# Merged rows to channels: transfers ahead of weight loads, turning ahead of splits, and one step a piece later

## The chip, the cores and the metric

The kernel runs on one core of one Trainium2 chip. The metric is the time of one execution on the device in microseconds (us). Three executions of the kernel before took 885.33, 885.78 and 892.01 us; their median is 885.78 us. A separate execution was profiled, and all rows and durations below come from that one.

## The reference: what is computed

Two layers, each with two halves, on 256 tokens of 1024 channels in float32. The first half mixes tokens:

```python
def _token_mixer(xn, ...):
    u, q, k, v, g_pool, g_attn = jnp.split(xn @ w_in, SPLITS, axis=-1)
    pool_out = ...        # centred means of u in 4 windows, minus u, times w_pool, times pool_scale
    attn_out = ...        # 12 heads in 3 dilated groups, merged by their softmax denominators
    merged = jax.nn.sigmoid(g_pool) * (pool_out @ w_a) + jax.nn.sigmoid(g_attn) * (attn_out @ w_b)
    return merged @ w_o

h = h + _token_mixer(_rmsnorm(h, norm1[layer]), ...)
h = h + _conv_ffn(_rmsnorm(h, norm2[layer]), w_up, conv_w, conv_b, w_down)
```

The second half is a gated MLP of width 2816 with a convolution over three tokens. At the end stands one more RMSNorm. The change lies between `merged` and `merged @ w_o`, with one small edit a little before it.

## The kernel before

**Three products for one.** Every float32 operand of a matmul is split into a high part, which ScalarE (ACT) makes by a cast, and a low part, which VectorE (DVE) makes by subtracting the high part from the operand. The product is then high by high, high by low and low by high, all on TensorE (PE). So each weight that arrives from memory has to pass ACT (line L194, tiles `wh`) and DVE (line L195, tiles `wl`) before PE can use it.

**The stream of weights.** The class `Weights` holds two lists that are laid out ahead of time: *loads*, each a transfer of 1 MB that SyncE (SP) issues (L131, tiles `raw`), and *pieces*, each half a load, in the order in which PE uses them. The raw tiles have three buffers, so a load has to wait until DVE has split both pieces of the load three places earlier. The split tiles have five buffers, so a split has to wait until PE is done with the piece five places earlier. Some pieces go to tiles that lie idle then (`slots`), such as the first three pieces of `w_up` (tiles `v1`, `ybig` and `at2`). `get` hands out the next piece and splits ahead by three.

In layer 0 the pieces around the change are: 62 to 65 (the first half of the attention gate's weights), 66 and 67 (`w_b`, first half), 68 to 71 (second half of the gate's), 72 and 73 (`w_b`, second half), 74 to 81 (`w_o`, eight chunks of 128 rows), and from 82 on `w_up`. Loads 37 to 40 are those of `w_o`, load 41 is the first of `w_up`. Layer 1 has the same order.

**What orders the work.** The order of instructions on each engine is settled when the program is built, by a scheduler that follows the order of the code and its own estimates; an engine then runs its list in order, and an instruction that waits holds up all that stand behind it on that engine. `issue_after(x)` makes what is traced in its block stand behind `x` in the list of the engine of `x`, and does nothing on other engines. `queue_behind(insts, n, first)` does that for the splits of `n` pieces from `first` on. SP's list holds all transfers, loads and others.

**From merged rows to channels.** `merged` comes out with tokens on the partitions, and `w_o` needs channels on the partitions. The second loop over `HALVES` does this for 512 channels at a time (n = 0 and n = 1). PE computes the gate (`gate`, L640, four pieces) and `attn_out @ w_b` (L640, two pieces held, first the rows t = 0, then t = 1). For each t DVE multiplies by the gate (L1129), adds the pool branch (L1132) and turns blocks of 32 by 32 (L661). `to_chunks` then stores the turned rows to memory (one transfer, L668, 512 KB, tile `turned`) and fetches them back in four transfers of 128 KB with channels on partitions (L671, tile `merged`). The first of the four waits for the store to land. ACT and DVE split the result into `m` (L677 and L678, two instructions each).

In n = 1 DVE's three steps stand behind the last L678 of n = 0 (`issue_after(last[1].ins)`).

**The product with `w_o`.** `residual_mm` (L558, L559, L560) takes chunks 0 to 3, which come from n = 0, for all four output tiles. Chunks 4 to 7, which come from n = 1, are held and worked off tile by tile: rows t = 0 with columns 0 to 511, t = 0 with the rest, then t = 1. After each tile DVE adds it to `h` (L418), and ACT takes the sum of squares (L420). When t = 0 is complete, POOL finishes the norm, DVE scales (L445), and PE turns the normed rows (L454, tile `xt_ps`); this stands in PE's list after the third tile and the first 256 columns of the fourth. Then comes the first product with `w_up`, which uses pieces 82 to 85 (`begin_mlp`).

**The steps between pieces.** The attention of the last two heads is cut into six steps: scores, turn, scores, weigh, turn, weigh. They are put between the eight pieces of `pool_out @ w_a` (L1100, by `places`), one after each piece but the two named there.

Of the kernel before, what the change touches and what calls it, by code (L numbers as in the profile page):

```python
# [94 lines left out]
class Weights:  # L95
# [8 lines left out]
    def __init__(self, tc, pool, idle):  # L104
        self.tc, self.nc, self.pool, self.idle = tc, tc.nc, pool, idle
        self.loads, self.pieces = [], []
        self.n_loaded, self.n_split, self.n_got = 0, 0, 0
        self.raw, self.split = {}, {}
        self.live = set()
        self.behind, self.later = (), []  # L110
        self.n_scaled, self.gains = 0, None

    def add(self, src, shape, cuts, tag=None):
# [9 lines left out]
    def load(self, upto):  # L123
        while self.n_loaded < min(upto, len(self.loads)):
            src, shape, tag = self.loads[self.n_loaded]
            name = f"raw{self.n_loaded}"
            if tag is None:
                t = self.pool.tile([P, *shape], F32, tag="raw", bufs=self.RAW, name=name)
            else:
                t = self.idle.tile([P, *shape], F32, tag=tag, name=name)  # L130
            self.last = self.nc.sync.dma_start(out=t, in_=src)  # L131
            self.raw[self.n_loaded] = t
            self.n_loaded += 1

# [89 lines left out]
def encoder(ctx, tc, x, w_in, w_pool, pool_scale, w_a, w_b, w_o, norm1, norm2, w_up, conv_w,  # L224
            conv_b, w_down, rel_bias, norm_f, onehot, edges, out):
    nc = tc.nc
# [9 lines left out]
    W = Weights(tc, wpool, big)  # L236
# [8 lines left out]
    def rows(w, r0, n=2, c0=0, width=1024, tag=None, pieces=2):  # L245

        src = w[r0 : r0 + n * P, c0 : c0 + width].rearrange("(k p) c -> p k c", p=P)
        h = n // pieces
        return W.add(
            src, (n, width), [((lambda t, j=j: t[:, j * h : (j + 1) * h, :]), (h, width)) for j in range(pieces)],  # L250
            tag,
        )

    first_up = []
    for l in range(DEPTH):
        for g in range(NG):
            c0 = C_V + g * 512
            slots = (("m2", 0, 2), ("m2", 1, 2), ("ybig",), ("at2",)) if g == 0 else ()
            for j in range(2):
                tag = "k1" if l == 0 and g == 1 and j == 0 else None  # L260
                W.use(rows(w_in[l], j * 512, 4, c0, 512, tag), slots[2 * j : 2 * j + 2])
        if l == 0:
            W.n_scaled = len(W.pieces)
        for c in range(3, -1, -1):
            W.use(cols(w_in[l], c * 256))
        for n, c in enumerate(PAIRS):
            pool = ([], [])
            if n == 1:
                pool = W.add(
                    w_pool[l].rearrange("g (k p) c -> p (g k) c", p=P), (8, 256),  # L270
                    [((lambda t, j=j: t[:, 4 * j : 4 * j + 4, :]), (4, 256)) for j in range(2)],
                )
                pool = (pool[:1], pool[1:])
            W.use(pool[0] + cols(w_in[l], C_Q + c * 256))
            W.use(pool[1] + cols(w_in[l], C_K + c * 256))
        for w, c0 in ((w_a[l], 0), (w_in[l], C_GP)):
            for c in (c0, c0 + 512):
                W.use(rows(w, 0, 4, c, 512) + rows(w, 512, 4, c, 512))
        for c in (0, 512):
            W.use(rows(w_in[l], 0, 4, C_GA + c, 512) + rows(w_in[l], 512, 4, C_GA + c, 512))  # L280
            W.use(rows(w_b[l], 0, 4, c, 512))
        for c in range(4):
            W.use(rows(w_o[l], c * 256))
        first_up.append(len(W.pieces))
        slots = (("v1",), ("ybig",), ("at2",))
        for j in range(2):
            W.use(rows(w_up[l], j * 512, 4, 0, 512), slots[2 * j : 2 * j + 2])
        for f in range(0, NF, 2):
            a = cols(w_up[l], f * P) if f >= ENTRY else []
            g = cols(w_up[l], DFF + f * P)  # L290
            W.use([a[0], g[0], a[1], g[1]] if a else g)
            if f >= LAG:
# [338 lines left out]
    def v_tile():  # L631
        return acc.tile([P, 512], F32, tag="acc", name="v_ps")
# [12 lines left out]
    def by_tokens(x2, n, at_once=1, then=None):  # L645

        ps = [mmp.tile([P, 512], F32, tag="mm", name="t_ps") for _ in range(2)]
        for i0 in range(0, n, at_once):
            held = [W.get() for _ in range(at_once)]
            for t in range(2):  # L650
                for i, piece in enumerate(held, i0):
                    v_sum(ps[t], x2, t, i, piece, n - 1)
            for i, _ in held:
                W.free(i)
            if then:
                then()
        return ps
# [5 lines left out]
    def to_chunks(y, z, x2):  # L663

        d = dram.tile([P, 4, 256], F32, tag="turned", bufs=2, name="turned")
        nc.sync.dma_start(out=d, in_=y.rearrange("p q c t j -> p q (c t j)"))  # L668
        for q in range(4):
            src = d[:, q].rearrange("(a i) x -> i a x", a=4)  # L670
            nc.sync.dma_start(out=z[32 * q : 32 * q + 32].rearrange("p a c t j -> p a (c t j)"), in_=src)  # L671
        for c in range(0, 4, 2):
            cs = slice(c, c + 2)
            src = z[:, :, cs].rearrange("p a c t j -> p a (c t) j")
            hi, lo = (p[:, cs].rearrange("p c t (a j) -> p a (c t) j", a=4) for p in x2)
            last = (
                nc.scalar.copy(out=hi, in_=src),  # L677
                nc.vector.tensor_sub(out=lo, in0=src, in1=hi.bitcast(F32)),  # L678
            )
        return last  # L680

    def two_parts(tag, name):

# [176 lines left out]
    for l in range(DEPTH):  # L860
# [25 lines left out]
        else:  # L886
            for g in range(NG):
                held = begun[0] if g == 0 else [W.get() for _ in range(4)]
                for t in range(2):
                    if g + t == 0:  # L890
                        ps = begun[1]
                    else:
                        ps = v_tile()
# [18 lines left out]
        for gi in range(3, -1, -1):  # L912
# [10 lines left out]
            cur, n = u, S + 2 * PAD  # L923
            sh = 1
            while sh < w:
# [3 lines left out]
                    out=nxt[:, :, 0:n], in0=cur[:, :, 0:n], in1=cur[:, :, sh : sh + n]  # L929
# [7 lines left out]
            if hw > 1:  # L937
# [5 lines left out]
                out=pd, in0=cur[:, :, o : o + S], scalar=1.0 / w, in1=u[:, :, PAD : PAD + S],  # L943
# [35 lines left out]
        q = big.tile([P, NH - HPG, 2, P], F32, tag="q1", name="q")  # L979
# [72 lines left out]
        for pair in ((0, 1), (2, 3)):  # L1052
            a, b = pair
            steps += [(scores, a), (turn, a), (scores, b), (weigh, a), (turn, b), (weigh, b)]

        def step():
            if steps:
                f, hh = steps.pop(0)
                f(hh)


        for m, c in enumerate(PAIRS):
            if m == 1:
                po2 = two_parts("m2", "po2")
# [5 lines left out]
            for n in range(4):  # L1070
                if m == 1:
                    next(pool_parts)
                src, rest = (halves(a) for a in proj(x2, 1 + (m != 1)))
                hd = 2 * c + n % 2
                scale = HD**-0.5 if n < 2 else 1.0
                if hd < HPG:
# [3 lines left out]
                        out=lo[:, hd], in0=src, scalar=scale, in1=hi[:, hd].bitcast(F32),  # L1080
# [3 lines left out]
                        out=lo[:, hd], in0=rest, scalar=scale, in1=lo[:, hd].bitcast(F32),  # L1084
                        op0=ALU.mult, op1=ALU.add,
                    )
                else:
# [3 lines left out]
                        out=o, in0=src, scalar=scale, in1=o, op0=ALU.mult, op1=ALU.add  # L1091
# [5 lines left out]
        pa = big.tile([P, 2, D], F32, tag="ybig", name="pa")  # L1097
        places = iter(range(KD))
        for cc in HALVES:
            ps = by_tokens(po2, 4, then=lambda: step() if next(places) not in (1, 6) else None)  # L1100
            for t in range(2):
                nc.scalar.copy(out=pa[:, t, cc], in_=ps[t])
        assert not steps
# [9 lines left out]
        for cc in HALVES:  # L1113
            th = gate()
            for t in range(2):
                nc.vector.scalar_tensor_tensor(
                    out=pa[:, t, cc], in0=th[:, t], scalar=1.0, in1=pa[:, t, cc],
# [3 lines left out]
        mh, ml = m2[:, 0], m2[:, 1]  # L1121
        z = big.tile([P, 2, 4, 4, 2, 32], F32, tag="q1", name="merged")
        for n, cc in enumerate(HALVES):
            th = gate()
            ps = by_tokens(at2, 2, 2)
            y = big.tile([P, 4, 4, 2, 32], F32, tag=("q0", "k0")[n], name="turned")
            for t in range(2):
                with tc.issue_after(last[1].ins) if n else ExitStack():
                    nc.vector.scalar_tensor_tensor(  # L1129
                        out=th[:, t], in0=th[:, t], scalar=1.0, in1=ps[t], op0=ALU.add, op1=ALU.mult  # L1130
                    )
                    nc.vector.tensor_add(out=th[:, t], in0=th[:, t], in1=pa[:, t, cc])  # L1132
                    turned = turn_blocks(y, t, th[:, t])
                last = (None, turned)
            ks = slice(4 * n, 4 * n + 4)
            last = to_chunks(y, z[:, n], (mh[:, ks], ml[:, ks]))
            if n == 0:

                W.queue_behind(last, 5, first_up[l] - 5)
        W.queue_behind((turned,), 4, first_up[l] - 4)  # L1140
        W.queue_behind(last, 4, first_up[l])

        x2 = two_parts("x", "x2")
        norm = Norm(to_channels(x2, acc, g2))
# [40 lines left out]
        held, ps = entry  # L1185
        first = keep_entry(ps)
        ps = v_tile()
# [6 lines left out]
        last = keep_entry(ps)  # L1194
# [99 lines left out]
```

## Time and profile before

| | us |
|---|---|
| median of three executions (lowest, highest) | 885.78 (885.33, 892.01) |
| the profiled execution | 887.53 |
| its span, first to last instruction | 885.7 |
| PE busy in the span | 868.5 |
| DVE busy | 661.9 |
| ACT busy | 509.3 |
| mean granted TensorE clock | 0.992 |

The profiled execution lasted 1.83 us longer than its span; that part lies outside of the first and last instruction. Times in the rows are counted from the start of the span. Rows of the timeline have the start, the duration, the engine, the line, the operation and the tiles written and read; in brackets stands the idle time before it and what ended that. Rows of the chain of work that ended last have the start, the share of that step in the chain, and what it is. A row of the waits names who waited, for whom, the total, how often, and the longest. Matmuls overlap: one of 512 columns is shown with 0.39 us, but the next starts 0.23 us later.

### The profile page before, as it was taken

The page shows a single profiled execution, that of the slowest core. Times are in us where ns is not written, and L with a number is a line of the kernel's source. Part 1 is how long each engine was busy: PE and PEld are TensorE (multiplying, and loading weights), DVE is VectorE, ACT ScalarE, POOL GpSimd, SP SyncE. Part 2 cuts the span into 40 slices and gives each one's busy share as a digit, 9 for nine tenths or more (in the row PEclk, how much of TensorE's full clock was granted, in tenths as well). Part 3 has the DMA queues.
Part 4 walks back from the last instruction along what each step waited for, and adds up shares of the span by engine and source line. Part 5 has one row for each costly group of instructions (what it writes and reads, how often), then busy time and mean ns, then how long its engine had stood idle before and what let it go on. Part 6 is the DMA issues. An engine that isn't in the chain of part 4 may idle for free.

```text
span 885.7 us, 12137 instructions
## 1 busy us (share of the span) xinstructions
PE 868.5 (98%) x4583; PEld 748.1 (84%) x4583; DVE 661.9 (75%) x1070; ACT 509.3 (57%) x847; POOL 31.0 (3%) x98
## 2 busy tenths in 40 slices
PE   9999999999899999999999999999997999999997
PEld 7888888888688888888888888988885888888886
DVE  7998786656669978878756988764556698887884
ACT  7657554544447766666545575454444477666663
POOL 1800000000010000000000000000000100000000
PEclk9999999999989999999999999999998999999999
DMA  9676544456745475465636474544576356646531
GB/s 332 236 236 219 179 156 161 142 178 207 257 142 191 143 229 198 145 235 192 236 120 233 148 237 145 172 160 143 190 235 194 127 181 219 209 145 234 192 142 48
DMA packets 116547, 165.86 MB, mean 187 GB/s; under 512 B 3640, under 2 KB 84224, under 8 KB 116488
## 3 DMA queue, kind: packets, MB, share of 16 engines
q1 hardware_dynamic: 116328, 164.81, 55.6%
q8 instruction: 36, 0.59, 0.3%
q10 hardware_dynamic: 160, 0.27, 0.1%
q14 instruction: 23, 0.19, 0.1%
HBM read 161.90 MB, written 3.17 MB: 186 GB/s over the span
## 4 chain that ended last, share of the span: by engine, by line
PE 92%; DMA 4%; DVE 2%; SPq 1%; ACT 1%; issue 0%; POOLq 0%; POOL 0%; ACTq 0%
PE proj_ps L516 45%; PE t_ps L640 14%; PE v_ps L640 6%; PE res_ps L558 6%; PE res_ps L559 6%; PE res_ps L560 6%; DMA merged<-turned 2%; PE v_ps L852 2%; PE pool_ps L516 1%; PE v_ps L759 1%; DMA turned<-turned 1%; PE pt_ps L1022 1%; PE o_ps L1043 1%; PE s_ps L993 1%; PE s_ps L988 1%; PE o_ps L1039 1%
## 5 line engine op out<-in xcount | busy, mean ns | idle before, releaser
L195 DVE TENSOR_TENSOR wl<-raw,wh 128x1024 fp32r<-128x1024 f32 x274 | 333.5, 1221 | 138.8 <-ACT wh L194 93.7
L194 ACT CAST wh<-raw 128x1024 fp32r<-128x1024 f32 x274 | 286.2, 1050 | 133.5 <-PE t_ps L640 60.2
L516 PE MATMUL proj_ps<-x,wh 128*128 128x512 f32 x1152 | 274.5, 390 | 0.0
L516 PEld LDWEIGHTS proj_ps<-x,wh 128*128 128x128 f32 x1152 | 213.1, 188 | 42.2
L516 PEld LDWEIGHTS proj_ps<-x,wl 128*128 128x128 f32 x1152 | 144.9, 191 | 3.6
L516 PE MATMUL proj_ps<-x,wl 128*128 128x256 f32 x1152 | 147.9, 283 | 0.0
L640 PE MATMUL t_ps<-wh,x 128*128 128x512 f32 x256 | 79.6, 390 | 0.0
L558 PE MATMUL res_ps<-wh,actq 128*128 128x512 f32 (+1 forms) x184 | 70.0, 380 | 0.0
L559 PE MATMUL res_ps<-wl,actq 128*128 128x512 f32 (+1 forms) x184 | 69.9, 380 | 0.0
L560 PE MATMUL res_ps<-wh,actk 128*128 128x512 f32 (+1 forms) x184 | 69.9, 380 | 0.0
L640 PEld LDWEIGHTS t_ps<-wh,x 128*128 128x128 f32 x256 | 48.1, 188 | 10.0
L640 PE MATMUL t_ps<-wl,x 128*128 128x512 f32 x128 | 49.8, 389 | 0.0
L640 PE MATMUL t_ps<-wh,po 128*128 128x512 f32 x128 | 42.7, 399 | 0.0
L558 PEld LDWEIGHTS res_ps<-wh,actq 128*128 128x128 f32 x184 | 34.6, 188 | 6.6
L559 PEld LDWEIGHTS res_ps<-wl,actq 128*128 128x128 f32 x184 | 34.6, 188 | 6.6
L560 PEld LDWEIGHTS res_ps<-wh,actk 128*128 128x128 f32 x184 | 34.6, 188 | 6.5
L558 PE MATMUL res_ps<-wh,m 128*128 128x512 f32 (+1 forms) x72 | 29.1, 404 | 10.2 <-ACT m L677 10.2
L1220 ACT ACTIVATE y<-y 128x256 f32<-128x256 f32 x44 | 18.2, 417 | 28.4 <-DVE y L1211 28.3
L427 POOL TENSOR_SCALAR ss<-ss 128x1 f32<-128x1 f32 x8 | 2.4, 302 | 812.7 <-ACT junk L420 812.7
L1207 ACT ACTIVATE y<-a,prm 128x256 f32<-128x256 f32 x36 | 21.6, 600 | 14.7 <-DVE a L553 14.7
L559 PE MATMUL res_ps<-wl,m 128*128 128x512 f32 (+1 forms) x72 | 28.4, 395 | 0.0
L640 PEld LDWEIGHTS t_ps<-wl,x 128*128 128x128 f32 x128 | 24.0, 188 | 4.9
(209 smaller groups left out, 1168.3 us busy)
## 6 DMA issues: line engine op xcount, KB each, us to landing
raw<-in_w_in_dram SPq DMA_DIRECT2D x58, 1024.0 KB, 5.6
raw<-in_w_up_dram SPq DMA_DIRECT2D x44, 1024.0 KB, 5.4
raw<-in_w_down_dram SPq DMA_DIRECT2D x22, 1024.0 KB, 4.8
raw<-in_w_a_dram SPq DMA_DIRECT2D x8, 1024.0 KB, 5.1
raw<-in_w_o_dram SPq DMA_DIRECT2D x8, 1024.0 KB, 6.5
raw<-in_w_b_dram SPq DMA_DIRECT2D x4, 1024.0 KB
raw<-in_w_pool_dram SPq DMA_DIRECT2D x2, 1024.0 KB
turned<-turned SPq DMA_DIRECT2D x4, 512.0 KB
```

The costliest lines, as they stand in the source:

```text
L194: lambda: nc.scalar.copy(out=h, in_=src),
L195: lambda: nc.vector.tensor_sub(out=l, in0=src, in1=h.bitcast(F32)),
L516: nc.tensor.matmul(out, w(k), x, start=(steps is first and k == 0), stop=(steps is last and k == nk - 1), skip_group_check=turns["rest"],)
L558: nc.tensor.matmul(ps, ah, wh, start=first, stop=False, skip_group_check=on)
L559: nc.tensor.matmul(ps, ah, wl, start=False, stop=False, skip_group_check=on)
L560: nc.tensor.matmul(ps, al, wh, start=False, stop=last, skip_group_check=on)
L640: nc.tensor.matmul(ps, x2[:, 2 * n + j, part, t, :], w[:, j, :], start=(n + m == 0), stop=(n == last and m == 5),)
L759: return nc.tensor.matmul(ps[t], a[:, k, t, :], w[:, k % 2, :], start=first, stop=last)
L852: nc.tensor.matmul(ps[t], a[:, k, t, :], w[:, j, :], start=(k + m == 0), stop=(k == KD - 1 and m == 2),)
L988: nc.tensor.matmul(ps[:, 0:256], a[:, hh, t, :], b[:, hh].rearrange("p t m -> p (t m)"), start=(m == 0), stop=(m == 2),)
L1207: nc.scalar.activation(y, a, AF.Identity, bias=b, scale=w1)
L1220: nc.scalar.activation(y2, y, AF.Square, scale=float(np.sqrt(0.044715)))
```

## The change

Four edits, all in the code around `to_chunks` but the last one.

1. `to_chunks` also returns the last of its four fetches (`there`). A new table `loads_behind` names loads that have to stand behind such a fetch in SP's list: the third and fourth load of `w_o` behind the fetches of n = 0, and the first three loads of `w_up` behind those of n = 1.
2. In n = 0, the next piece to be split (piece 71 in layer 0) stands behind the turning of t = 1 in DVE's list.
3. In n = 1, the last five pieces of `w_o` (77 to 81) stand behind the turning of t = 1 in DVE's list; before, four pieces from `first_up - 4` (78 to 81) did. They still stand behind the split of n = 0.
4. `places` leaves out piece 5 in place of piece 6, so the second `turn` step comes after piece 6 instead of after piece 5.

```diff
 def load(self, upto):
     ...
-            self.last = self.nc.sync.dma_start(out=t, in_=src)
+            held = self.loads_behind.get(self.n_loaded)
+            with self.tc.issue_after(held.ins) if held else ExitStack():
+                self.last = self.nc.sync.dma_start(out=t, in_=src)
 ...
-        first_up.append(len(W.pieces))
+        first_up.append((len(W.pieces), len(W.loads)))
 ...
 def to_chunks(y, z, x2):
     ...
         for q in range(4):
             src = d[:, q].rearrange("(a i) x -> i a x", a=4)
-            nc.sync.dma_start(out=z[32 * q : 32 * q + 32]..., in_=src)
+            there = nc.sync.dma_start(out=z[32 * q : 32 * q + 32]..., in_=src)
     ...
-        return last
+        return there, last
 ...
-            ps = by_tokens(po2, 4, then=lambda: step() if next(places) not in (1, 6) else None)
+            ps = by_tokens(po2, 4, then=lambda: step() if next(places) not in (1, 5) else None)
 ...
-            last = to_chunks(y, z[:, n], (mh[:, ks], ml[:, ks]))
+            there, last = to_chunks(y, z[:, n], (mh[:, ks], ml[:, ks]))
+            piece, load = first_up[l]
             if n == 0:
-                W.queue_behind(last, 5, first_up[l] - 5)
-        W.queue_behind((turned,), 4, first_up[l] - 4)
-        W.queue_behind(last, 4, first_up[l])
+                W.queue_behind((turned,), 1)
+                W.loads_behind.update({load - 2: there, load - 1: there})
+                W.queue_behind(last, 5, piece - 5)
+            else:
+                W.queue_behind((turned,), 5, piece - 5)
+                W.loads_behind.update({load: there, load + 1: there, load + 2: there})
+                W.queue_behind(last, 4, piece)
```

As built, the changed program has the same instructions on every engine as the program before. In each layer their order differs in these places alone. SP: the store of n = 0 stands ahead of the second load of `w_o`, the fetches of n = 0 ahead of the third, the store and the fetches of n = 1 ahead of the first two loads of `w_up`. DVE: the splits of pieces 71 and 72 stand behind the turning of t = 1 in n = 0, that of piece 77 behind the turning of t = 1 in n = 1; in the norm after `w_o` the split into `at2` stands behind the first addition to `h`, and the third addition ahead of two of the scalings. ACT: piece 57 is split ahead of the copies of the second `turn` step, and one sum of squares stands ahead of the split of piece 85. PE: the second `turn` stands one piece later, and the first matmul with a low part of `m` stands third instead of fifth in the product with `w_o`.

More of the change, by code (lines that the diff above doesn't have):

```diff
@@ L110, in __init__ @@
         self.behind, self.later = (), []
+        self.loads_behind = {}
         self.n_scaled, self.gains = 0, None
@@ L670, in to_chunks @@
             src = d[:, q].rearrange("(a i) x -> i a x", a=4)
-            nc.sync.dma_start(out=z[32 * q : 32 * q + 32].rearrange("p a c t j -> p a (c t j)"), in_=src)
+            there = nc.sync.dma_start(
+                out=z[32 * q : 32 * q + 32].rearrange("p a c t j -> p a (c t j)"), in_=src
+            )
         for c in range(0, 4, 2):
```

## The prediction

> **What bounds the kernel now.** I read the page first, then who waited on PE, then the busy time and clock by stretch, then the chain around the largest wait, then DVE's and SP's rows there.
>
> ```profile
> PE 868.5 (98%) x4583; PEld 748.1 (84%) x4583; DVE 661.9 (75%) x1070; ACT 509.3 (57%) x847; POOL 31.0 (3%) x98
> PE 92%; DMA 4%; DVE 2%; SPq 1%; ACT 1%; issue 0%; POOLq 0%; POOL 0%; ACTq 0%
> ...
> PE res_ps L558 <- ACT m L677: 10.2, 2, 5.8
> ```
>
> PE is busy for 98% of the span and carries 92% of the chain. Of 17 us in which it isn't, 10.2 are two waits of one kind: the product with w_o, which has used up chunks 0 to 3, waits for ACT's split of the second half of the merged rows. The next longest waits on PE are under 1 us and lie at the start. So the change can win something here and nowhere else. The stretches around the two waits:
>
> ```profile
> 228.30:239.30 11.00, 11.00 (x49) 8.80 (x47) 9.45 (x11) 4.22 (x4) 0.00 (x0) 1.00 0.62 213
> 239.30:243.80 4.50, 0.07 (x2) 0.05 (x1) 0.07 (x1) 0.72 (x2) 0.00 (x0) 0.91 1.09 317
> 243.80:250.00 6.20, 6.20 (x15) 4.82 (x16) 5.44 (x7) 4.21 (x5) 0.00 (x0) 0.51 0.38 120
> 250.00:256.30 6.30, 6.30 (x35) 5.43 (x34) 3.26 (x6) 1.45 (x4) 1.13 (x3) 1.00 0.84 284
> 675.50:681.30 5.80, 0.03 (x1) 0.00 (x0) 0.01 (x1) 0.66 (x2) 0.00 (x0) 0.88 1.07 330
> 681.30:687.00 5.70, 5.69 (x14) 4.49 (x15) 4.94 (x6) 4.26 (x5) 0.00 (x0) 0.52 0.27 91
> ```
>
> After the bounds come length, then busy time with counts for PE, PEld, DVE, ACT and POOL, then granted clock, DMA share and GB/s. PE stands still for 4.4 and 5.8 us (first and fifth stretch with a clock below 1.00), and behind each wait it runs at a clock of 0.51 and 0.52: there the matmuls follow each other at 0.43 us instead of 0.23. So each wait costs its length and then, in 6.1 us that hold 14 matmuls, another 6.1 - 14 x 0.23 = 2.9 us. All in all 4.4 + 2.9 + 5.8 + 2.9 = 16.0 us: the most the change can win. What leads to the first wait is in the chain:
>
> ```profile
> 226.18 0.63 ACT m L677
> 226.83 0.56 DVE m L678
> ...
> 228.13 0.60 DVE gates L1129
> 228.72 1.14 DVE wl L195
> 229.86 0.61 DVE gates L1132
> 230.50 0.71 DVE turned L661
> 231.21 0.58 DVE gates L1129
> 231.81 0.70 DVE gates L1132
> 232.54 0.72 DVE turned L661
> 233.28 2.96 DMA turned<-turned
> 236.25 0.33 SPq L671
> ...
> 237.57 5.41 DMA merged<-turned
> 243.08 0.63 ACT m L677
> ```
>
> DVE makes both turnings of n = 1 with a weight split (1.14 us) between them; the store takes 2.96 us; the last fetch takes 5.41 us to land. In SP's list a load of 1 MB stands right ahead of the fetches. And n = 1 itself starts behind the split of n = 0, whose turning has two weight splits in it:
>
> ```profile
> 211.89 1.23 DVE L195 TENSOR_TENSOR wl<-raw,wh 128x1024 fp32r<-128x1024 f32 x1 [0.29 <-ACT wh L194]
> 213.03 0.68 DVE L1129 SCALAR_TENSOR_TENSOR gates<-gates,t_ps 128x512 f32<-128x512 f32 x1
> 213.62 1.22 DVE L195 TENSOR_TENSOR wl<-raw,wh 128x1024 fp32r<-128x1024 f32 x1
> ```
>
> **Part by part, layer 0.**
>
> *Turning of n = 0 (edit 2).* PE's sums for t = 1 are there at 212.1 (they release ACT's cast at 212.16). Without splits between, L1129 to store takes what t = 1 of n = 1 takes above, 233.28 - 231.21 = 2.07 us: store at 214.2, not 216.22. The two splits (1.14 us each in sequence) run right behind; piece 71's is done at 215.4 instead of 213.1. PE needs piece 71 at 220.1 (two pieces of 2.72 us ahead of the b-products at 222.8), so this cover is 4.7 us. The second w_o load moves with it, from 213.14 to 215.4; its first split is at 223.5.
>
> *Fetches of n = 0 (edit 1).* The store takes 2.96 to 3.25 us (layer 0 and 1, n = 1 and n = 0): last fetch issued near 218.7. It lands 4.76 us later as before, to 6.26 as in layer 1: 223.5 to 225.0, with a load ahead of it as before. ACT is not free until 224.57 (a cast of 1.04 us from 223.53 stands ahead), and DVE's split ahead ends at 225.8. So L678 runs from 225.8, not 226.83, and n = 1 can start at 227.05, not 228.13: of 2 us, 1.1 are left.
>
> *Turning of n = 1 (edit 3).* With no split between: 0.60 + 0.70 + 0.72 for t = 0, 2.07 for t = 1: store at 231.1 instead of 233.28. Five splits follow; piece 77 is done at 232.4, and PE needs it at 236.4. ACT's casts keep their places.
>
> *Fetches of n = 1 (edit 1).* Last issue at 231.1 + 2.96 + 1.32 = 235.4. What a fetch takes with no load ahead, no row shows. From above: the 5.41 and 5.56 us of now. From below: 2.96 us, which the store of the same 512 KB takes. A megabyte at the 317 GB/s of that stretch is 3.3 us, so the load's removal speaks for the lower end; I take 3.5. Landing at 238.9, ACT 0.1 later, PE 0.67 after that (243.08 to 243.75): 239.7, where PE is out of work at 239.3. The wait falls from 4.4 to 0.4 us, and the slow clock with it.
>
> *Loads behind the fetches.* The first two loads of w_up go out near 235.9 and 236.4 instead of 229.89 and 235.52. At 317 to 400 GB/s they land about 241 and 244. In DVE's list the splits into v1 and ybig stand ahead of the first addition to h, and the split into at2 ahead of the second. With casts of 1.04 us and splits of 1.14 us: second addition at 245.3 to 246.4. From there to the first turning of normed rows it takes 3.4 us (252.36 to 255.7 now: sum of squares, POOL, two scalings of 0.40). PE, which doesn't slow down, wants to turn at 249.1. So the cover that is there now (0.6 us) is gone, and a new wait of 0 to 0.8 us stands there; I take 0.4. Loads after these wait for splits that PE paces; they come earlier in absolute terms.
>
> Layer 0: 4.4 - 0.4 + 2.9 - 0.4 = **6.5 us**.
>
> **Layer 1** has the same rows 436.2 us later, up to the fetches of n = 0, which land at 663.34 and hold up n = 1 (DVE idle for 2.05 us). Sooner by 2 us, they land at 661.4; n = 1 stores at 667.5 instead of 670.54, lands at 675.4, PE goes on at 676.1 instead of 681.3. 5.8 - 0.6 + 2.9 - 0.4 = **7.7 us**.
>
> **Edit 4.** PE has no wait in these steps, so nothing can be won. The second turn has 2.7 us to its use in place of 5.5: transposes end at 169.5, ACT's cast of piece 57 stands ahead of the copies (to 169.9), DVE's split ahead of its three (0.34 each), which end at 172.2; PE wants them at 172.3. 0 to 0.3 us a layer; I take 0.1.
>
> **Sum.** 6.5 + 7.7 - 0.2 = 14.0 us, against the profiled execution's own 887.53: **873.5 us**. That execution is 1.75 us above the median shown; I do not take this off, since the rows do not say where it arises, but it belongs to the lower end.
>
> The Trainium skill (TensorE: Matmul & The Clock Gate, part 1) says that the clock is halved after one idle window of about 3.4 us, and that the windows run free. The trace agrees as far as it goes: both waits are longer, both are followed by half the clock, and waits of 0.3 us are not. By that rule a wait of 4.4 us is caught in some executions only, so that the median before would hold less than 5.8 us of slow clock, and a wait left over below 3.4 us would cost its length alone. By the opposite, a rest of 2 us would cost 5.
>
> **Rivals.**
>
> *The fetches take as long as now* (5.4 to 5.6 us with DMA share above 1 in the wait). Only the earlier issue is won, 2.2 and 3.0 us; waits of 2.2 and 2.8 us stay. At full clock behind them 887.5 - 5.2 - 5.8 = 876.5; with half the clock 882.3. For it: the fetches of rows of 1 KB stayed slow in layer 1 with loads behind them as well.
>
> *The norm becomes the wait.* If the first w_up loads land 2 us later than I reckon (load 42 at 246), the second addition is at 248.2 and PE waits 2.4 us at the turning in each layer: 873.5 + 4 = 877.5. Against it: the sibling stage behind w_down has the same splits between its additions and no wait on PE.
>
> *Slower.* The same place, further: DVE's list puts the splits of late loads ahead of the additions to h, so it stands still until loads land that now queue behind the fetches. PE turns at 256.3 now; the change loses when load 42 lands after 250.6, 14 us after its issue. Each microsecond beyond costs one per layer, and at 252.5 it is 891. The longest landing in the rows here is 7.6 us (first fetch of n = 0 in layer 1 to its last landing), so this needs twice that.
>
> *It does not do what it says:* the order as built shows it does, but if DVE's gain were lost behind ACT's cast at 223.5 and nothing else moved, 886.
>
> **How the numbers follow.** My forecast 0.66 (870 to 876.5), fetches as now 0.15, norm 0.11, slower 0.05, nothing 0.03. The range of 8 in 10 takes in all of the first, most of the second at full clock and the norm: 869.5 to 880; the low end is the most that can be won (16) and the profiled execution's excess (1.75). Within 1%, about what a measurement of this kernel can tell from no change, means 876.9 to 894.6. Faster by more: 0.64 of the first, 0.08 of the second, 0.05 of the third: 0.77. Slower by more: 0.05. Same: 0.18.
>
> **What would show it.** PE's waits on ACT's L677 (new line number, same tiles) below 1 us each in the waits; a clock of 1.00 through both stretches; stores 2 to 3 us sooner; last fetch to landing 3 to 4 us; a new wait of xt_ps on DVE below 1 us. Wrong would be: fetches still above 5 us, a half clock that stays, or a wait of DVE on the loads of w_up that grows into PE's.

## The result and the profile after

| | before | after |
|---|---|---|
| first comparison, median of six and six (us) | 886.83 | 875.13 (873.40 to 878.07) |
| its ratio, 95% interval | | 0.9864 [0.9835, 0.9893] |
| later comparison, median of 17 and four | 886.33 | 873.16 (872.87 to 873.41) |
| its ratio | | 0.9855 [0.9837, 0.9874] |
| profiled execution (first comparison) | 887.53 | 875.60 |
| its span | 885.7 | 873.8 |

The kernel is 1.4% faster. The later comparison is that of the run `as_changed` below, the same kernel once more. From the page of the kernel after: busy time and instructions, the shares of the chain that ended last, and who waited longest on PE.

```profile
PE 864.0 (99%) x4583; PEld 744.5 (85%) x4583; DVE 662.2 (76%) x1070; ACT 510.2 (58%) x847; POOL 32.5 (4%) x98
PE 95%; DMA 2%; DVE 1%; ACT 1%; issue 0%; SPq 0%; POOL 0%; POOLq 0%; ACTq 0%; DVEq 0%
...
PE xt_ps L457 <- DVE xn L448: 3.3, 2, 1.7
```

Both waits on ACT's split of the merged rows (10.2 us) are gone from the list. In their place stands a new one, 3.3 us in two, of PE's turning of the normed rows on DVE's scaling. The stretches of the windows view after (length, then busy time and count of PE, PEld, DVE, ACT, POOL, granted clock, DMA share, GB/s):

```profile
239.30:243.80 4.50, 4.50 (x21) 3.69 (x21) 1.11 (x2) 1.76 (x2) 0.00 (x0) 1.00 1.05 384
243.80:250.00 6.20, 4.86 (x28) 4.08 (x26) 5.46 (x7) 3.69 (x7) 1.31 (x3) 1.00 0.78 272
...
664.50:675.50 11.00, 11.00 (x49) 8.93 (x48) 5.77 (x7) 5.28 (x7) 0.00 (x0) 1.00 0.88 303
```

The first stretch is the one in which PE stood still before; it is now busy throughout, and the clock is 1.00 everywhere. SP's rows around the second half in layer 0 (start, duration, what is issued):

```profile
230.75 0.34 SPq L671 DMA_DIRECT2D turned<-turned  x1
233.36 1.75 SPq L674 DMA_DIRECT2D merged<-turned  x4
235.21 14.23 SPq L134 DMA_DIRECT2D raw<-in_w_up_dram  x5
```

The store goes out at 230.75 (before: 233.28), the fetches follow it directly, and the loads of `w_up` come behind them. ACT's first split of the result starts at 237.79 instead of 243.08.

**The account.** Marks that PE passes in both kernels tell where the 11.9 us of the span arose:

| from one mark to the next (layer 0, layer 1) | before (us) | after (us) | difference |
|---|---|---|---|
| start to the first matmul with w_o, layer 0 | 228.28 | 227.86 | -0.42 |
| from there to the first matmul behind the turning of normed rows | 28.39 | 23.05 | -5.34 |
| to the second turning of the product with w_up (`a_turn`) | 17.09 | 17.22 | +0.13 |
| to the first matmul with w_o, layer 1 | 390.73 | 390.71 | -0.02 |
| the same stretch of layer 1 | 29.45 | 22.99 | -6.46 |
| the same product of layer 1 | 17.07 | 17.24 | +0.17 |
| to PE's last matmul | 169.00 | 169.01 | +0.01 |

Outside of the product with `w_o` and what directly follows it nothing changed but the 0.42 us of the first line, which arise in the first 15 us, long before the changed code. The marks of two single executions are compared here. In layer 0 the wait (4.43) and the half clock (6.83 us at half speed, less the 0.73 us of it in which PE still waited, make 3.05 us) are gone, and the new wait of 1.66 is there; that makes 5.82, and the turnings took 0.23 us longer (PE follows DVE's scalings at close distance there; that this is the reason was not tested). In layer 1 it is 5.77 + 2.73 - 1.65 - 0.23 = 6.62. 0.2 us in each layer is not placed.

What leads to the new wait, in the timeline of the kernel after, layer 0 (ACT, then DVE, then PE; in brackets the idle time before and what ended it):

```profile
242.04 1.05 ACT L197 CAST v<-raw 128x1024 fp32r<-128x1024 f32 x1 [3.11 <-DMA raw<-in_w_up_dram]
...
243.12 1.23 DVE L198 TENSOR_TENSOR v<-raw,v 128x1024 fp32r<-128x1024 f32 x1 [3.39 <-ACT v L197]
244.27 1.22 DVE L198 TENSOR_TENSOR ybig<-raw,ybig 128x1024 fp32r<-128x1024 f32 x1
245.40 0.68 DVE L421 TENSOR_TENSOR h<-res_ps,h 128x512 f32<-128x512 f32 x1
246.00 1.21 DVE L198 TENSOR_TENSOR at<-raw,at 128x1024 fp32r<-128x1024 f32 x1
247.14 0.68 DVE L421 TENSOR_TENSOR h<-res_ps,h 128x512 f32<-128x512 f32 x1
...
250.32 0.83 PE L457 MATMUL xt_ps<-ident,xn 128*128 128x128 f32 x4 [1.66 <-DVE xn L448]
```

The first load of `w_up` was issued at 235.21 and is split from 242.04 on, 6.83 us later. DVE stood idle for 3.39 us until then, with the additions to `h` behind the splits in its list, and PE's turning is 1.66 us late.

### The profile page after: what moved, and what is told of

Same layout as the page of the kernel before. It is cut to its first block, busy times and chain, and to the rows that moved or that the text cites. A ratio compares the mean times of both kernels' runs of the same rounds, so it can differ in the third digit from the quotient of the medians.

```text
span 873.8 us, 12139 instructions
## 1 busy us (share of the span) xinstructions
PE 864.0 (99%) x4583; PEld 744.5 (85%) x4583; DVE 662.2 (76%) x1070; ACT 510.2 (58%) x847; POOL 32.5 (4%) x98
## 4 chain that ended last, share of the span: by engine, by line
PE 95%; DMA 2%; DVE 1%; ACT 1%; issue 0%; SPq 0%; POOL 0%; POOLq 0%; ACTq 0%; DVEq 0%
PE proj_ps L519 46%; PE t_ps L643 16%; PE v_ps L643 6%; PE res_ps L563 5%; PE res_ps L561 5%; PE res_ps L562 5%; PE v_ps L857 2%; PE v_ps L764 1%; PE pool_ps L519 1%; PE pt_ps L1027 1%; PE o_ps L1048 1%; PE s_ps L998 1%; DMA raw<-in_w_up_dram 1%; PE xt_ps L457 1%; PE s_ps L993 1%; PE o_ps L1044 1%
## 5 line engine op out<-in xcount | busy, mean ns | idle before, releaser
L643 PEld LDWEIGHTS t_ps<-wh,po 128*128 128x128 f32 x128 | 24.1, 188 | 4.7
L563 PE MATMUL res_ps<-wh,m 128*128 128x512 f32 (+1 forms) x72 | 26.5, 369 | 0.0
```

Of the source, the lines that this page charges most:

```text
L563: nc.tensor.matmul(ps, al, wh, start=False, stop=last, skip_group_check=on)
L643: nc.tensor.matmul(ps, x2[:, 2 * n + j, part, t, :], w[:, j, :], start=(n + m == 0), stop=(n == last and m == 5),)
```

## The experiments

Each run is compared with the kernel before on the same chip. The first four take the change apart in two ways: by engine (DVE's turning, SP's transfers) and by half (n = 0, n = 1). All four leave the fourth edit out.

### DVE's part alone

Shown against the changed kernel:

```diff
             if n == 0:
                 W.queue_behind((turned,), 1)
-                W.loads_behind.update({load - 2: there, load - 1: there})
                 W.queue_behind(last, 5, piece - 5)
             else:
                 W.queue_behind((turned,), 5, piece - 5)
-                W.loads_behind.update({load: there, load + 1: there, load + 2: there})
```

> DVE's part alone: the turning of both halves goes ahead of the weight splits (edits 2 and 3), SP's order of loads and fetches and the step (edits 1 and 4) stay as in the kernel before. Theory (the gain is the two fetch waits and the half clock behind them, and the order of the transfers matters by itself): stores 2.2 us (layer 0) and 3 us (layer 1) sooner, fetches still 5.4 us or more from issue to landing, so waits of 2.2 and 2.8 us in place of 4.4 and 5.8, no half clock behind them since both are shorter than 3.4 us, no wait at the turning of normed rows: 887.5 - 5.2 - 5.8 = 876.5. Rival A (any wait of 2 us or more is followed by half the clock): 882.3. Rival B (the order of the transfers does nothing, the earlier store is the whole gain): waits near 0, 873 or less.

Measured: 876.42 us against 885.22, ratio 0.9911 [0.9884, 0.9938]. The chain around the wait of layer 0 in this kernel (start, length, what):

```profile
230.82 2.82 DMA turned<-turned
...
234.98 4.62 DMA merged<-turned
...
239.70 0.63 ACT m L682
...
240.37 0.50 PE res_ps L561
```

The store is as early as in the full change, but a load of 1 MB was issued at 231.93, ahead of the fetches, and the last of these takes 4.62 us. PE waits for 1.40 us here and for 1.93 in layer 1, at full clock behind both. Rival B falls, since the waits are not near 0. Rival A is not tested here, since both waits are below 2 us; the 2.08 us of the second half's run, further down, stand against it. In one of the four executions (880.44 us, mean clock 0.996 instead of 0.999) some half clock seems to have come back; its rows aren't known.

The run is not DVE's part alone, though, and its expectation was wrong in that. No line for SP was set, but the scheduler ordered SP's list anew along with DVE's:

```profile
230.82 0.34 SPq L671 DMA_DIRECT2D turned<-turned  x1
231.93 0.37 SPq L134 DMA_DIRECT2D raw<-in_w_up_dram  x1
233.66 1.75 SPq L674 DMA_DIRECT2D merged<-turned  x4
235.51 0.39 SPq L134 DMA_DIRECT2D raw<-in_w_up_dram  x1
```

In the kernel before, loads were issued at 229.89 and 235.52, both ahead of the fetches (from 236.25). Here one of the two stands ahead of them and one behind. For n = 0 SP's order is that of the full change. So the run holds DVE's part and a share of SP's, and what DVE's order is worth by itself was not measured.

### SP's part alone

```diff
             if n == 0:
-                W.queue_behind((turned,), 1)
                 W.loads_behind.update({load - 2: there, load - 1: there})
                 W.queue_behind(last, 5, piece - 5)
             else:
-                W.queue_behind((turned,), 5, piece - 5)
+                W.queue_behind((turned,), 4, piece - 4)
                 W.loads_behind.update({load: there, load + 1: there, load + 2: there})
```

> SP's part alone: the loads go behind the fetches of both halves (edit 1), DVE's order and the step stay as before. Theory: stores as before in n = 1 of layer 0 (up to 2 us sooner in layer 1, where n = 1 waits for the fetches of n = 0), store to ACT's split of m 7.0 us instead of 9.8, so waits of 1.7 and 0.7 to 2.7 us; the loads of w_up land about 2.4 us later than in the changed kernel, so the turning of normed rows waits about 2 us in each layer; no half clock: 887.5 - (4.4 + 2.9 - 3.7) - (5.8 + 2.9 - 3.7) = 879. Rival A (a wait of 2 us costs half a clock too): 885. Rival B (the fetches are slow by their rows of 1 KB, not by the load ahead of them): waits as before, 887.

Measured: 876.64 us, ratio 0.9903 [0.9884, 0.9921]. The store of n = 1 goes out at 233.13, as late as before, but from the last fetch's issue (237.06) to ACT's split (240.02) it takes 2.96 us, where the kernel before took 5.51. PE waits for 1.15 and 1.16 us on the fetches and for 0.31 and 0.49 on the turning of normed rows, at full clock. Rival B is refuted: the fetches were slow because of the loads ahead of them. In this run DVE's list is as before up to the split of the second half, so it is SP's part alone. The waits at the turning were expected at 2 us and are at most a quarter of that, although the loads go out 2.4 us later than in the full change: here the first load took 5.3 us and not 6.8. That made the profile above suspect, and the last group of runs takes it up.

### By halves

The first half's run keeps the lines for `n == 0` and puts `queue_behind((turned,), 4, piece - 4)` back for n = 1; the second half's run keeps the lines for n = 1 and leaves out the two new ones for n = 0.

> The parts for n = 0 alone: turning of n = 0 ahead of splits, third and fourth load of w_o behind the fetches of n = 0; n = 1 and the step as before. Theory: n = 1 starts 1.0 us (layer 0) and 1.7 us (layer 1) sooner, nothing else: waits of 3.4 and 4.1 us. Whether they are followed by half a clock is not settled by that: without it 887.5 - 1.0 - 1.7 - 5.8 = 879, with it in layer 1 alone 882, in both 885. A wait of 4.4 us with half a clock behind it in the kernel before and one of 4.1 us without would say that chance (where a window of 3.4 us starts) decides. Rival (the first half decides, since the second stands behind it in every list): waits under 2 us, below 876.

> The parts for n = 1 alone: one more split behind the turning of n = 1, the first three loads of w_up behind its fetches; n = 0 and the step as before. Theory: store 1.1 us sooner and fetch 2.8 to 3.1 us shorter, so waits of 0.5 and 1.5 us, and waits of about 2 us at the turning of normed rows, since the loads of w_up land later while DVE's splits of them stand ahead of the additions to h: 887.5 - (4.4 + 2.9 - 2.7) - (5.8 + 2.9 - 3.3) = 877.5. With the first half's run this adds up to more than the whole change gives, because the half clock can only be removed once. Rival (both halves are needed): above 881.

Measured: first half 884.41 us, ratio 0.9997 [0.9982, 1.0011]; second half 875.62 us, ratio 0.9896 [0.9873, 0.9918]. With the first half alone PE waits for 3.76 and 3.90 us instead of 4.43 and 5.77, and the half clock stays behind both. The time is the same within the measurement, although the waits are 2.5 us shorter; where that went isn't shown. The waits of the kernel before differ between executions: with the fourth edit alone, the last run below, they are 5.18 and 4.54. With the second half alone the waits are 0 and 2.08 us (and 0.87 in n = 0 of layer 1, 0.30 and 0.62 at the turning), without half clock, in a profiled execution of 877.97 us, the slowest of the four. The expectation had 877.5 with about 2 us at the turning, which did not come. So it isn't true that both halves are needed. n = 1 carries 9.6 us of the 13.2 that the whole change gives in the later comparison; n = 0 is worth nothing that can be measured by itself, and the rest only on top of n = 1.

The two runs by engine don't add up either: 8.8 (DVE, with its share of SP's) and 8.6 (SP) against 13.2 us for both together. Part of the reason is that share. The other is in the profiles: either run gets both waits below 2 us, and with that the half clock goes (5.8 us in the profiled execution before), which can go only once. What the second part then finds is 3.3 and 2.3 us of waits on the fetches.

### From which wait on the clock is halved

The half-clock stretches of all profiles (but the one at the end, behind PE's last matmul) are 3.41 or 6.83 us long, and within an execution their starts lie a multiple of 3.413 us apart (243.02 and 679.93 in the kernel before: 128 times). So the stretches of that length ahead of a slow one can be cut out exactly. The windows view for the first half's run:

```profile
238.94:242.35 3.41, 0.61 (x3) 0.18 (x1) 0.24 (x1) 0.00 (x0) 0.00 (x0) 1.00 0.96 277
242.35:245.76 3.41, 2.45 (x6) 1.92 (x7) 2.29 (x3) 3.12 (x5) 0.00 (x0) 0.50 0.77 265
245.76:249.17 3.41, 3.41 (x10) 2.64 (x9) 2.83 (x4) 1.81 (x2) 0.00 (x0) 0.50 0.21 57
249.17:252.58 3.41, 3.41 (x17) 2.78 (x16) 2.18 (x3) 0.74 (x3) 0.37 (x1) 1.00 0.88 302
```

And for the second half's run, around its longest wait:

```profile
668.90:672.32 3.42, 1.88 (x9) 1.22 (x7) 1.73 (x2) 0.38 (x2) 0.00 (x0) 1.00 0.88 246
672.32:675.73 3.41, 2.87 (x11) 2.10 (x12) 1.29 (x2) 1.44 (x3) 0.00 (x0) 1.00 1.04 399
```

And two single lines, the first of the kernel before, behind its wait in layer 0, the second of the kernel after, around its wait of 1.66:

```profile
243.02:246.43 3.41, 2.68 (x6) 2.11 (x7) 2.52 (x4) 3.35 (x5) 0.00 (x0) 0.50 0.64 212
...
247.18:250.59 3.41, 1.75 (x15) 1.48 (x13) 2.67 (x6) 1.33 (x3) 1.06 (x3) 1.00 0.91 314
```

A stretch in which PE is busy for 0.61 of 3.41 us is followed by half the clock; one with 1.88 or 1.75 is not. A slow stretch that PE doesn't fill (2.45, and 2.68 in the kernel before) is followed by another slow one; one that it fills is followed by the full clock.

### The splits of w_up behind the additions

Three kernels hold the four splits of pieces 82 to 85 back until additions to `h` have been traced. In `splits_between` two stand behind the first addition and two behind the second, in `splits_1_3` one and three; in `splits_later` all four stand behind the second. The core of the first, with `N0, N1 = 2, 2`:

```diff
+        def added(t, m, cc, ps):
+            then = norm.add(t, m, cc, ps)
+            if t == 0:
+                n = (N0, N1)[m]
+                W.queue_behind((norm.added,), n, W.hold)
+                W.hold += n
+                W._split(W.hold)
+            ...
+            return then
-        run(residual_mm(lambda k: (mh[:, k], ml[:, k]), KD, norm.add, fill=begin_mlp))
+        run(residual_mm(lambda k: (mh[:, k], ml[:, k]), KD, added, fill=begin_mlp))
```

> The changed kernel with the first four splits of w_up taken out from ahead of the first addition to h: two behind the first addition, two behind the second, in ACT's and DVE's lists. Theory (the 1.66 us that are left at the turning of normed rows come from DVE's splits of late loads ahead of the additions): the additions come as soon as PE's sums do, the waits of 1.66 us go to 0 to 0.5 and nothing else is near, so 875.1 - 2.3 to 3.3 = 872 to 873. Rival A (the norm's own chain of squares, POOL and scalings is as long as PE's cover): waits stay, 875. Rival B (the splits are now late for the product with w_up): the wait moves there, 874 to 876.

> As the run with two splits behind each addition, but with one behind the first addition and three behind the second, so that the second addition waits for one load alone. Theory: since both additions wait for nothing but PE's sums and the first load's split, the waits at the turning go to 0: 872, or 0.3 us better than with two and two. Rival (the three splits stand ahead of the scalings, 3 x 1.14 us): a wait of 1 to 2 us at the turning, 875.

> The changed kernel with all four splits of w_up behind the second addition to h and the first scalings. Theory: the first turning of normed rows waits no more, but 4 x 1.14 = 4.6 us of splits now stand ahead of the scaling of the second rows, so the second turning, or the first product with w_up, waits about 2 to 3 us in each layer: 876 to 878. Rival (any place behind the additions will do): 872.

Measured on one chip, where the kernel before took 885.54: 871.81, 873.23 and 881.65 us (ratios 0.9847 [0.9832, 0.9861], 0.9863 [0.9848, 0.9878], 0.9953 [0.9938, 0.9969]). The first two have no wait at the turning left. The expectation for `splits_1_3`, 872 us or 0.3 better than two and two, was wrong: it is 1.4 us slower. DVE's scalings start at 249.69 in layer 0 instead of 248.53, behind three splits. No wait of PE is listed, but right behind the scalings its turning of the second rows takes 0.72 us instead of 0.35 and the six products after it 1.76 instead of 1.48. `splits_later` was expected at 876 to 878 with waits of 2 to 3 us, and has them:

```profile
PE xt_ps L461 <- DVE xn L452: 5.9, 2, 3.0
```

What this expectation missed is the clock. The stretch that holds the wait, and the two behind it, in the windows view of this kernel:

```profile
250.61:254.02 3.41, 0.45 (x4) 0.36 (x3) 3.41 (x6) 0.72 (x2) 0.00 (x0) 1.00 0.76 248
254.02:257.43 3.41, 3.41 (x11) 2.79 (x10) 2.24 (x5) 1.50 (x5) 0.56 (x3) 0.50 1.03 363
257.43:260.84 3.41, 3.41 (x18) 2.80 (x18) 1.67 (x4) 0.34 (x1) 0.62 (x2) 1.00 0.02 7
```

A wait of 2.96 us, shorter than the stretch, is enough: 11 matmuls are done in the next one instead of 18.

### The fourth edit, and the wait that came and went

> The changed kernel with the fourth edit undone (the step after piece 5, as in the kernel before). Theory: no wait of PE's lies in these steps in either kernel, so nothing changes: 875 within 0.5. Rival (a later second turn costs 0.1 to 0.3 us a layer): 874.5.

This is the changed kernel with `(1, 6)` in `places` again. Measured beside the three kernels with moved splits: 872.85 us, ratio 0.9859 [0.9845, 0.9874], and no wait at the turning above 0.2 us, where the changed kernel's profile had 1.66 in each layer. Either the fourth edit makes the wait, or the first profile was not typical. Four more kernels on one chip tell these apart: the changed kernel, the last one again, the same with two splits behind each addition, and the kernel before with the fourth edit alone.

> The changed kernel itself, beside the kernels it is to be compared with. Its profiled execution had the first load of w_up land 6.7 to 6.8 us after its issue in both layers, and 1.66 us of wait at the turning of normed rows behind that; in six other kernels with the loads behind the fetches it took 5.1 to 5.5 us. Theory (the landing differs from execution to execution, not by the kernel): 5.1 to 5.5 us here too, the wait 0 to 0.3, 872.5 to 873.5. Rival (edit 4 makes it late, as the kernel without it had no such wait): 875, wait 1.6 and landing 6.7 again.

> The changed kernel with the fourth edit undone, once more beside the changed kernel. Theory: the same as the changed kernel within 0.5, whatever the loads do. Rival (edit 4 costs time): 2 us less than the changed kernel.

> The fourth edit undone, and two splits of w_up behind each of the first two additions to h. Theory: where the first load lands 5.3 us after its issue, the turning waits for nothing, and the place of the splits is worth 0 to 0.5: 872 to 873. Where it lands 6.8 us after, it is worth 2 to 3 against the changed kernel. Rival (edit 4 and the place of the splits add up): 870.

> The kernel before with the fourth edit alone. Theory: same as before within 0.1%. Rival (0.1 to 0.3 us a layer lost at the second turn): up to 0.6 slower.

Measured, with the kernel before at 886.33:

| kernel | us | ratio, 95% interval | first load of w_up, issue to split, layer 0 and 1 | wait at the turning |
|---|---|---|---|---|
| as_changed | 873.16 | 0.9855 [0.9837, 0.9874] | 5.20, 5.57 | 0.10, 0.36 |
| step_again | 872.98 | 0.9857 [0.9838, 0.9876] | 5.21, 5.10 | 0.06, 0 |
| between_step | 871.66 | 0.9840 [0.9822, 0.9858] | 5.31, 5.46 | 0, 0 |
| step_alone | 885.38 | 0.9987 [0.9974, 1.0001] | | |

The fourth edit is worth nothing that can be measured, with the rest of the change or without it. So the wait of 1.66 us is not in every execution of the kernel. How often it comes isn't known: the other five of the first comparison took 873.40 to 878.07 us and have no rows, while all four of `as_changed` took 872.87 to 873.41, so it may have been more than the one there. The chain of the changed kernel's second profile shows how near to the edge it is, though:

```profile
235.25 5.17 DMA raw<-in_w_up_dram
...
240.44 1.06 ACT v L197
...
241.53 1.23 DVE v L198
...
243.81 0.68 DVE h L421
...
248.19 0.49 DVE xn L448
...
248.73 0.83 PE xt_ps L457 x4
```

The chain that ends last leads from the load to the turning: with a landing after 5.2 us PE still comes to its turning at about the same time as DVE. In this pair of profiles the rest goes to PE: 6.83 - 5.20 = 1.63 us of later landing made 1.66 - 0.10 = 1.56 us of longer wait. Why it landed late is only partly visible. In the first profile 253 GB/s moved from 236.7 to 238.4, in the second 323; and when the first load was there, 1.7 MB of weights had been moved since its issue, in the other profiles 1.3 to 1.46 MB. So more rows of the loads behind it were served before its own last ones. Whether that is due to the chip or to something else in that execution stays open.

Four executions of `between_step` (871.60 to 872.20) lie below all four of `as_changed` (872.87 to 873.41). The place of the splits was expected to be worth 0 to 0.5 us where the first load lands as early as here. The waits account for 0.46 of the 1.5 us. The rest shows on PE around the turning, first in `as_changed`:

```profile
248.73 0.83 PE L457 MATMUL xt_ps<-ident,xn 128*128 128x128 f32 x4
249.32 0.36 PE L561 MATMUL res_ps<-wh,m 128*128 128x256 f32 x1
```

And in `between_step`:

```profile
249.07 0.38 PE L461 MATMUL xt_ps<-ident,xn 128*128 128x128 f32 x2
249.21 0.37 PE L565 MATMUL res_ps<-wh,m 128*128 128x256 f32 x1
249.42 0.38 PE L461 MATMUL xt_ps<-ident,xn 128*128 128x128 f32 x2
249.55 0.37 PE L566 MATMUL res_ps<-wl,m 128*128 128x256 f32 x1
```

Four turnings take 0.59 us to the next matmul in the first; in the kernel before it was 0.36. In the second they stand three matmuls later in PE's list and in two pairs, and take 0.14 us a pair. Counted from the first turning to the second half's split products (the tile `a_turn`), PE needs 11.83 us in `as_changed` and, with three matmuls of 0.12 us added that it has already done, 11.46 in `between_step`: 0.37 a layer, twice 0.37 and 0.46 make 1.2 of the 1.5 us. `between_step` is the fastest version found, with `splits_between`, which has the fourth edit as well and took 871.81 us on another chip (ratios 0.9840 and 0.9847, their intervals overlap).

## Why the prediction was right

The forecast was 873.5 us (869.5 to 880); 875.13 and 873.16 were measured. That it lies so close to the second number is partly luck. The 14.0 us were taken off one execution of 887.53, and the medians differ by 11.7 and 13.2 us, from 886.83 and 886.33. The half clock in that execution lasted 6.83 us behind both waits; with the fourth edit alone, which is worth nothing measurable, it was 6.83 and 3.41. So both the start and the gain of the sum were somewhat too large. The mechanism was right. Its steps, in times of the rows, for layer 0 (the two last lines by the marks above):

| step | forecast | first profile | second profile |
|---|---|---|---|
| store of n = 0 | 214.2 | 213.93 | 213.96 |
| L678 (now L683) of n = 0 | 225.8 | 225.33 | 225.36 |
| store of n = 1 | 231.1 | 230.75 | 230.79 |
| last fetch issued | 235.4 | 234.69 | 234.72 |
| from there to the split of m | 3.6 | 3.10 | 2.96 |
| wait left on the fetches | 0.4 | 0 | 0 |
| half clock | none | none | none |
| first two loads of w_up there | 241, 244 | 242.0, 244.6 | 240.4, 243.2 |
| second addition to h | 245.3 to 246.4 | 247.14 | 245.54 |
| new wait at the turning | 0.4 (0 to 0.8) | 1.66 | 0.10 |
| saved in layer 0 | 6.5 | 5.2 | 6.8 |
| saved in layer 1 | 7.7 | 6.3 | 7.4 |

*Turning and fetches (edits 1 to 3).* Right in place and size. All starts are 0.3 to 0.7 us early; 0.4 of it the changed kernel's executions were ahead before any of these steps. In layer 1 the store of n = 1 is at 661.74, and with the 5.65 us that PE was ahead by then, by the marks, 667.39 (forecast 667.5). The bound from above on a fetch, 5.4 us, was what it costs with the loads ahead (4.6 with one of the two, in DVE's part alone); the value near the lower bound was the right choice, and slightly too high: 3.0 and not 3.5. The waits left over were taken as 0.4 and 0.6 and are 0 and 0.

*The new wait.* The mechanism was forecast with its place, its cause in DVE's list and its lost cover of 0.6 us. Its size is the term that was wrong against the first profile: 1.66 instead of 0.4 in each layer. The failing input is the landing of the first load, "about 241", which was 242.0 because the load took 6.8 us; in the second profile it took 5.2, and the wait is below what was forecast. The sum of the forecast, 14.0 us, compares with 11.9 between the first two profiled executions and with 14.6 between the same one of before and the second. The rival in which the norm becomes the wait was priced rightly too, a microsecond of PE for each of later landing; the first profile, with its loads 0.6 to 1 us late, went a part of that way.

*Edit 4.* 0.1 us a layer was taken; PE passes the marks around these steps within 0.04 us of the kernel before, and the times of both pairs of runs agree within their intervals. So it is nearer to 0, though 0.1 a layer is less than the times could show.

*The half clock.* Right for the result: the longest wait left in the profiles of the kernel after is 1.66 us, and none was followed by half the clock. One of its ten executions, 878.07 us, has a mean clock of 0.997 where the others have 0.998 to 1.000; some half clock may have come back there, and its rows aren't known. Wrong was what the prediction drew from the rule about one idle window. The Trainium skill (TensorE: Matmul & The Clock Gate, part 1) gives a window of about 3.4 us that runs free, and the starts on a grid of 3.413 us agree with that. But the conclusion that a wait of 4.4 us would be caught in some executions only isn't borne out. All 17 executions of the kernel before in the later comparison have a mean clock of 0.991 to 0.994. The longest stretches seen, 6.83 us at half the clock behind one wait and 3.6 at the end of the span, take 5.2 us of clock, which leaves 0.994. So the 12 executions at 0.991 to 0.993 had half the clock behind both waits; for the five at 0.994 this can't be told. And a wait below 3.4 us doesn't always cost its length alone: 2.96 us was followed by half the clock in both layers. The window need not be idle from end to end.

*The other rivals.* The fetches as long as now: DVE's part alone comes nearest to that case, with one load ahead of the fetches in place of two, and fetches of 4.6 and 5.3 us. It came out at 876.4 us, where the rival at full clock had 876.5, but by another sum: waits of 1.40 and 1.93 instead of 2.2 and 2.8, and about 1 us a layer in which PE was slower around the turning, which isn't followed up here. This rival needs a load ahead of the fetches, and the change takes it away. Slower: the second load would have had to be there at 250.6, 6 us later than in the worse profile.

## What to carry to other kernels

Where a small store and fetch sits between two stages, look in the issuing queue for large loads right ahead of it: taking them away brought the fetches from 5.4 to 3.0 us and gave 8.6 us, as much as bringing the store forward by 2.5 us and taking away one of the two (8.8). Read the order of the transfers from the rows of each run, since an edit to one engine's list can move another's. Then look at who waits for the load that was moved back: here DVE's splits of it stand ahead of additions that the next stage needs, and the kernel now sits at the edge where each microsecond of later landing is one of PE. When a wait on PE is followed by half the clock, shortening it by a part may give nothing (3.8 and 3.9 us left: same time), and getting it to about 2 us gives more than its length; two edits that each do so don't add up.

## What the runs showed of the hardware

- The clock can be halved behind a wait that is shorter than a stretch of the grid of 3.413 us: with PE busy for 0.61, 0.45 and 0.45 of 3.41 us it was (waits of 3.76, 2.96 and 2.96), with 1.75 and 1.88 it was not. Between these no profile has a case.
- A slow stretch is prolonged by another when PE stands still for a part of it: 0.73 us of wait left (2.68 busy, the kernel before) was enough, and with PE busy throughout it ended. At full clock a stretch with 1.75 busy was not followed by a slow one, so a slow stretch took more work to end than a fast one to keep.
- A load of 1 MB landed after 5.1 to 5.6 us in most profiles and after 6.7 to 6.8 in one, with the same queue ahead of it and a second load issued 0.5 us behind. In the late case 1.7 MB of weights had been moved when the first load was complete, in the others 1.3 to 1.46. The Trainium skill (DMA: Bandwidth & Descriptors, Why a DMA increments its semaphore by 16 and not by 1) says that a transfer is spread over up to 16 engines and is there only when all of them have counted; the rows don't contradict that, but no row here says which engine was late.
